# Second MLP product: blocks go on in the same PSUM banks and straight into four output blocks, gate on the sum, first loads ahead of stores

## The chip, the cores and the metric

The kernel runs on one core of one Trainium2 chip. The metric is the device time of one execution in microseconds (us), the median over several runs. A profile is one further execution with the hardware profiler; its own time stands beside its span below.

## What is computed

The reference is one layer of a diffusion backbone block over 1024 latent tokens of width 1024 (a recurrent branch and a Fourier branch, merged), and then the part that matters here:

```python
def sq_relu_mlp(h, w1, w2):
    return jnp.square(jax.nn.relu(h @ w1)) @ w2
...
x = x + gt2 * sq_relu_mlp(modulate(rms_norm(x, g_mlp[i]), sh2, sc2), w1[i], w2[i])
...
return rms_norm(x, g_final)
```

The first MLP product is 1024 x 1024 by 1024 x 4096, the second 1024 x 4096 by 4096 x 1024. gt2 is one row of 1024 factors, the same for all tokens. All inputs are float32.

## The kernel before

Each float32 product is made of three matmuls in the type float32r: an operand is split into a high part (a ScalarE copy that rounds) and a low part (the VectorE difference, both at line 98 in `split`), and `passes` multiplies high by high, high by low and low by high. One matmul is 128 x 128 by 128 x 512.

The MLP runs as block products with seven instead of eight multiplications for a 2 x 2 block product (Strassen in Winograd's form). The first product (class `Pair`, 16 pairs of output rows, lines 902 to 1005) leaves its 32 results as rows of `act_d` in DRAM. For each pair seven products of 12 matmuls each (line 958) go into three PSUM banks, A, B and C; `out3` and `out4` (lines 999 and 992) add the last bank to a sum on VectorE, and `put_out` squares the positive part (line 1004) and stores it (line 1005). A bank is free for other use once that sum has been read.

The second product (class `Mlp2`, line 1017) takes 28 of the 32 rows of the hidden width in three chunks of 5, 5 and 4 blocks k (each block two hidden tiles of 128), and the last four plainly. For each block `load` brings four tiles x, y, z, w from DRAM, each a half of activations and a half of w2 (256 KB each). For each chunk there are seven units u, one for each of the seven products; `split` makes the operands of a unit, `sums` the sums that a later unit needs, `mm` does 12 matmuls for each block into two PSUM tiles of two banks, and `evac` reads them into a page in SBUF. In the loop of `run` the work of step i is recorded as: evac of unit i - 1, loads of the next chunk, split for unit i + 1, sums for unit i + 2, matmuls of unit i.

Before the change each unit has its own PSUM tiles and its own two pages (`acc`, 14 pages): ScalarE copies in the first chunk, VectorE adds in the others (line 1096). At the end `comb` (line 1107) makes the four output blocks out of the seven, 14 sums of 128 x 1024, and `gate` (line 1113) multiplies them by gt2 on GpSimd, 16 halves. The plain part multiplies its four w2 tiles by gt2 (line 1119), and for each of the eight output tiles 24 more matmuls run (line 1179), their result is added to the residual x2 (lines 1163, 1167), and `finish` normalises and stores a tile (lines 1011 to 1015). The last tile is finished in two halves (lines 1261 to 1269).

The order of instructions on TensorE, VectorE and ScalarE in this stage is the order in which the code records them (`tc.manual_schedule`). The order on SyncE, which issues all loads and stores, is set by the framework's scheduler; each load waits until its page is free and, at most eight being under way, for an earlier one. Lines 1252 and 1253 are the passage from the first product to the second:

```python
            mlp2.begin()
            pr[NP - 1].out4()
            psum_pool("psum2", 4)
            mlp2.run()
```

`begin` loads x and z, splits all five blocks of unit 0, loads y and makes the five sums for unit 1. Pages come from the pools `pg` (24, tag s), `yp` (17, tag y) and `wp` (tags wr, wh, wl).

Of the kernel before, what the change touches and what calls it, by code (L numbers as in the profile page):

```python
# [50 lines left out]
def block_kernel(es: ExitStack, tc: tile.TileContext, a, out):  # L51
# [695 lines left out]
    with tc.tile_pool(name="yp", bufs=17, reuse_waits="tile") as yp:  # L747
# [158 lines left out]
        class Pair:  # L906
            def __init__(self, n):
                self.n, self.w = n, {}
# [74 lines left out]
            def p7(self):  # L983
                self.f2 = page([P, T])
# [32 lines left out]
        class Mlp2:  # L1017
# [3 lines left out]
            RING = ("wr",) * 4 + ("y",) * 3 + ("wh", "wl") * 3 + ("s",) * 4  # L1021

            def __init__(self):
                self.units = [(c, u) for c in range(len(self.CHUNKS)) for u in range(7)]
                self.src = [{n: [None] * g for n in "xyzws"} for _, g in self.CHUNKS]
                self.op, self.ps, self.acc, self.slot = {}, {}, [[] for _ in range(7)], 0
# [8 lines left out]
            def load(self, c, names, new=page, ks=None):  # L1035
                n0, g = self.CHUNKS[c]
                for k in ks or range(g):
                    for n in names:
                        r, ca, cb, d = self.SRC[n]
                        t = self.src[c][n][k] = new([P, 2 * HB])  # L1040
                        f = 2 * (n0 + k)
                        dma(t[:, 0:HB], act_d[f + ca][:, r * HB:(r + 1) * HB])
                        dma(t[:, HB:], a["w2"][(f + cb) * P:(f + cb + 1) * P, d * HB:(d + 1) * HB])

            def split(self, i):
# [3 lines left out]
                p, self.op[i] = self.src[c], []  # L1049
                for k in range(self.CHUNKS[c][1]):  # L1050
# [4 lines left out]
                    else:  # L1055
                        split(p["_syyzwx"[u]][k], hi, lo)
                    self.op[i].append((hi, lo))

            def sums(self, i):
# [3 lines left out]
                p = self.src[c]  # L1063
                for k in range(self.CHUNKS[c][1]):
                    x, y, z, w = (p[n][k] for n in "xyzw")
# [12 lines left out]
            def mm(self, i):  # L1078
                self.ps[i] = [mm_ps() for _ in range(2)]
                op, t = self.op.pop(i), [h for ps in self.ps[i] for h in halves(ps)]  # L1080
                for k, hl in enumerate(op):
                    for j in range(4):
                        m = [q[:, j * P:(j + 1) * P] for q in hl]
                        for n, (l, r) in enumerate(passes(m, [q[:, HB:] for q in hl])):
                            PE.matmul(t[j], l, r, start=k == 0 and n == 0, stop=k == len(op) - 1 and n == 2)  # L1085

            def evac(self, i):
# [3 lines left out]
                for j, ps in enumerate(self.ps.pop(i)):  # L1091
                    if c == 0:
                        self.acc[u].append(ypage([P, 2 * HB]))
                        S.activation(self.acc[u][j], ps, AF.Copy)
                    else:
                        V.tensor_tensor(self.acc[u][j], self.acc[u][j], ps, ALU.add)  # L1096

            def begin(self):
                self.load(0, "xz", ypage, range(2))
                self.load(0, "xz", page, range(2, 5))  # L1100
                self.split(0)
                self.load(0, "y")
                self.sums(1)

            def comb(self, d, s0, s1, op):
                for j in range(2):
                    V.tensor_tensor(self.acc[d][j], self.acc[s0][j], self.acc[s1][j], op)  # L1107

            def gate(self, u, d):
                for j in range(2):  # L1110
                    t = self.acc[u][j].rearrange("p (a b) -> p a b", b=HB)
                    for h in range(2):
                        G.tensor_tensor(t[:, h], t[:, h], gt2[:, d * HB:(d + 1) * HB], ALU.mult)  # L1113
# [246 lines left out]
```

## Time and profile before

| | |
|---|---|
| median of 3 runs | 1471.16 us (1470.81 to 1471.35) |
| profiled execution, its own time | 1469.69 us |
| span of its profile | 1467.9 us |
| TensorE (PE), busy | 1390.6 us, 95% |
| VectorE (DVE), busy | 1058.0 us, 72% |
| ScalarE (ACT), busy | 611.2 us, 42% |
| GpSimd (POOL), busy | 123.6 us, 8% |
| granted TensorE clock, mean | 0.983 of full speed |

PE is TensorE's matmuls, PEld its weight loads, SPq SyncE's queue. The span runs from the first to the last instruction; the time of an execution has 1.79 us more. A matmul row shows about 0.39 us from start to end, but matmuls overlap: one starts every 0.23 us. Rows of VectorE overlap a little as well, so the pitch of several in a row is read from a merged row (x5). An arrow "<-" names what ended a wait.

### The profile page before, as it was taken

The numbers are of one execution on the slowest core, as the hardware profiler recorded it, in microseconds if no ns is written. First come the engines' busy times: TensorE is split into PE (matmuls) and PEld (weight loads), VectorE is DVE, ScalarE is ACT, GpSimd is POOL, SyncE is SP. The second block draws the span as 40 slices with busy tenths as digits, with TensorE's granted clock in tenths as the row PEclk, the third lists the DMA queues.
The fourth block names the chain that finished last, engine by engine and source line by source line (L and its number), as shares of the span: only waits on it lengthen the run. The fifth ranks groups of instructions, "written<-read, shape, count | busy, mean of one in ns | idle before, by whom it ended". The sixth has DMA issues, their size and how long they took to land. (4 is left out here: it accounts for less than half of the span.)

```text
span 1467.9 us, 16270 instructions
## 1 busy us (share of the span) xinstructions
PE 1390.6 (95%) x6352; PEld 1131.4 (77%) x6352; DVE 1058.0 (72%) x1209; ACT 611.2 (42%) x753; POOL 123.6 (8%) x62
## 2 busy tenths in 40 slices
PE   4999999999999999999996899999995999999995
PEld 3888788888888878788774678888884888888884
DVE  7664648888887998645656676666665847959998
ACT  7453246665676557321244312222222355333403
POOL 0000000000000000000001100000000320602573
PEclk9999999999999999999998999999998999999998
DMA  8432711333133324648422333332317352042322
GB/s 328 187 115 90 255 49 51 131 131 130 49 126 132 118 80 158 200 132 305 166 86 86 100 129 115 115 115 102 102 61 252 120 181 69 27 149 87 117 84 115
DMA packets 62540, 188.90 MB, mean 129 GB/s; under 512 B 6979, under 2 KB 7387, under 8 KB 62463
## 3 DMA queue, kind: packets, MB, share of 16 engines
q1 hardware_dynamic: 62463, 187.86, 37.1%
q8 instruction: 50, 0.82, 0.2%
q14 instruction: 27, 0.22, 0.0%
HBM read 150.60 MB, written 37.23 MB: 128 GB/s over the span
## 5 line engine op out<-in xcount | busy, mean ns | idle before, releaser
L321 PE MATMUL mm<-pg,wh 128*128 128x512 f32 x1120 | 308.3, 396 | 0.5 <-DVE pg L98 0.5
L321 PEld LDWEIGHTS mm<-pg,wh 128*128 128x128 f32 x1120 | 204.6, 189 | 43.7 <-DVE pg L98 1.0
L958 PE MATMUL bk<-pg,wh 128*128 128x512 f32 x720 | 225.9, 395 | 1.9 <-DVE wr L297 1.1
L321 PE MATMUL mm<-pg,wl 128*128 128x512 f32 x560 | 175.4, 394 | 0.0
L958 PEld LDWEIGHTS bk<-pg,wh 128*128 128x128 f32 x720 | 135.0, 188 | 34.5 <-DVE wr L297 2.1
L958 PE MATMUL bk<-pg,wl 128*128 128x512 f32 x360 | 141.6, 393 | 0.0
L98 DVE TENSOR_TENSOR wl<-wr,wh 128x1024 fp32r<-128x1024 f32 (+2 forms) x73 | 81.6, 1121 | 75.5 <-ACT wh L98 75.5
L98 ACT ACTIVATE wh<-wr 128x1024 fp32r<-128x1024 f32 (+2 forms) x73 | 71.0, 976 | 147.6 <-PE mm L321 67.0
L321 PEld LDWEIGHTS mm<-pg,wl 128*128 128x128 f32 x560 | 105.3, 188 | 24.3
L98 ACT ACTIVATE pg<-pg 128x1024 fp32r<-128x1024 f32 (+4 forms) x86 | 75.7, 901 | 64.5 <-PE mm L1085 13.3
L98 ACT ACTIVATE wh<-pg 128x1024 fp32r<-128x1024 f32 x48 | 50.2, 1061 | 125.7 <-PE bk L958 52.6
L98 DVE TENSOR_TENSOR pg<-pg,pg 128x1024 fp32r<-128x1024 f32 (+4 forms) x71 | 81.0, 1157 | 20.0 <-ACT pg L98 19.9
L859 PE MATMUL mm<-pg,pg 128*128 128x512 f32 x384 | 91.9, 397 | 0.0
L958 PE MATMUL bk<-pg,pg 128*128 128x512 f32 x264 | 72.5, 425 | 19.2 <-ACT pg L98 15.1
L859 PEld LDWEIGHTS mm<-pg,pg 128*128 128x128 f32 x384 | 71.0, 188 | 17.9 <-DVE g L893 2.2
L958 PEld LDWEIGHTS bk<-pg,pg 128*128 128x128 f32 x264 | 52.8, 205 | 35.9 <-ACT pg L98 19.0
L958 PEld LDWEIGHTS bk<-pg,wl 128*128 128x128 f32 x360 | 67.6, 188 | 16.0
L98 DVE TENSOR_TENSOR wl<-pg,wh 128x1024 fp32r<-128x1024 f32 x48 | 58.0, 1223 | 28.0 <-ACT wh L98 28.0
L1074 POOL TENSOR_TENSOR pg<-pg,pg 128x512 f32<-128x512 f32 x14 | 37.5, 2676 | 476.8 <-DVE pg L1072 476.8
L842 POOL TENSOR_TENSOR wr<-pg 128x512 f32<-128x512 f32 x4 | 5.7, 1424 | 810.5 <-ACT pg L823 800.5
L776 PE MATMUL mm<-pg,wh 128*128 128x512 f32 x256 | 70.0, 394 | 1.7 <-ACT pg L98 1.7
L1085 PE MATMUL mm<-pg,pg 128*128 128x512 f32 x224 | 69.7, 392 | 0.0
(279 smaller groups left out, 2659.1 us busy)
## 6 DMA issues: line engine op xcount, KB each, us to landing
wr<-in_win SPq DMA_DIRECT2D x36, 512.0 KB, 4.5
wr<-in_w SPq DMA_DIRECT2D x35, 512.0 KB, 3.6
pg<-in_wm SPq DMA_DIRECT2D x32, 512.0 KB, 8.1
wr<-in_wm SPq DMA_DIRECT2D x32, 512.0 KB, 3.7
act_d<-pg SPq DMA_DIRECT2D x32, 512.0 KB, 2.9
pg<-act_d SPq DMA_DIRECT2D x56, 256.0 KB, 4.8
pg<-in_w SPq DMA_DIRECT2D x56, 256.0 KB, 5.2
pg<-in_x SPq DMA_DIRECT2D x16, 512.0 KB, 8.2
```

The source lines that it names most:

```text
L98: return S.activation(hi, src, AF.Copy), V.tensor_tensor(lo, src, f32(hi), ALU.subtract)
L321: PE.matmul(ps[:, h * HB:(h + 1) * HB], l[:, k, :], r[:, h * HB:(h + 1) * HB], start=k == 0 and i == 0, stop=k == KT - 1 and i == 2)
L776: PE.matmul(ps[:, h * HB:(h + 1) * HB], l[:, k, :], r[:, h * HB:(h + 1) * HB], start=k == 0 and i == 0, stop=k == KT - 1 and i == 2)
L842: G.tensor_tensor(t34[:, 0], b22, b12, ALU.subtract)
L859: PE.matmul(ps, l, r, start=k == 0 and j == 0, stop=k == KT - 1 and j == 2)
L958: PE.matmul(ps, l, r, start=first and k == 0 and i == 0, stop=k == 3 and i == 2, skip_group_check=not first)
L1074: G.tensor_tensor(z[:, HB:], w[:, HB:], y[:, HB:], ALU.subtract)
L1085: PE.matmul(t[j], l, r, start=k == 0 and n == 0, stop=k == len(op) - 1 and n == 2)
```

## The change

- A unit of the second product that goes on from an earlier sum now accumulates on the PSUM tiles of two units before (units 2, 4 and 6 on those of unit 0, unit 3 on those of unit 1; table `ON`). The reordered units are then read straight into four output blocks (table `ACC`; units 2 and 4 subtract, table `SUB`). Eight pages take the place of 14; the combinations at the end are gone.
- `sums` makes other sums, all on VectorE: y + z, y - x, then halves w - y, z - y, y - z and w - y. The last one needs y's right half alone, and the left half of y is loaded once more for the seventh unit.
- gt2 multiplies the sum of an output tile (one product of 128 x 1024 on VectorE) and no longer the blocks and the plain w2 tiles; GpSimd has no work left in this stage.
- The loads of x, z and y of the first chunk are recorded inside the last pair, with higher priority; the splits of unit 0 are recorded as two blocks, then `out4`, then three blocks, then the sums for unit 1.
- The next chunk's tiles are loaded in steps 3 to 6 as x, z, y, w, and w of the first chunk before the loop. Output tiles are finished in the order 0 to 7 instead of 4 to 7, 0 to 3.

```diff
-            RING = ("wr",) * 4 + ("y",) * 3 + ("wh", "wl") * 3 + ("s",) * 4
+            RING = ("wr",) * 4 + ("y",) * 6 + ("wh", "wl") * 3 + ("s",)
+
+            PAGE = "_yyxzwy"
+            ACC = ((0, 0), (1, 1), (0, 1), (0, 1), (1, 1), (0, 0), (1, 0))
+            ON, SUB = (2, 3, 4, 6), (2, 4)
...
                     if u == 1:
-                        p["s"][k] = page([P, 2 * HB])
-                        V.tensor_tensor(p["s"][k], x, y, ALU.subtract)
+                        V.tensor_tensor(y, y, z, ALU.add)
                     elif u == 2:
-                        V.tensor_tensor(y, y, z, ALU.add)
+                        V.tensor_tensor(y, y, x, ALU.subtract)
                     elif u == 3:
-                        V.tensor_tensor(y, y, x, ALU.subtract)
+                        V.tensor_tensor(xl, wl, yl, ALU.subtract)
                     elif u == 4:
-                        G.tensor_tensor(z[:, HB:], w[:, HB:], y[:, HB:], ALU.subtract)
+                        V.tensor_tensor(zl, zl, yl, ALU.subtract)
+                        V.tensor_tensor(zr, yr, zr, ALU.subtract)
                     elif u == 5:
-                        G.tensor_tensor(x[:, 0:HB], w[:, 0:HB], y[:, 0:HB], ALU.subtract)
+                        V.tensor_tensor(yr, wr, yr, ALU.subtract)
+                        self.load_act(y, c, k, 1, 1)
...
-                self.ps[i] = [mm_ps() for _ in range(2)]
+                c, u = self.units[i]
+                self.ps[i] = self.ps[i - 2] if u in self.ON else [mm_ps() for _ in range(2)]
...
-                            PE.matmul(t[j], l, r, start=k == 0 and n == 0, stop=k == len(op) - 1 and n == 2)
+                            PE.matmul(t[j], l, r, start=u not in self.ON and k == 0 and n == 0,
+                                      stop=k == len(op) - 1 and n == 2, skip_group_check=u in self.ON)
...
-                for j, ps in enumerate(self.ps.pop(i)):
-                    if c == 0:
-                        self.acc[u].append(ypage([P, 2 * HB]))
-                        S.activation(self.acc[u][j], ps, AF.Copy)
+                d = self.ACC[u]
+                for j, ps in enumerate(self.ps[i]):
+                    if (d, j) not in self.acc:
+                        t = self.acc[d, j] = ypage([P, 2 * HB])
+                        S.activation(t, ps, AF.Copy, scale=-1.0 if u in self.SUB else 1.0)
                     else:
-                        V.tensor_tensor(self.acc[u][j], self.acc[u][j], ps, ALU.add)
+                        t = self.acc[d, j]
+                        V.tensor_tensor(t, t, ps, ALU.subtract if u in self.SUB else ALU.add)
 
             def begin(self):
-                self.load(0, "xz", ypage, range(2))
-                self.load(0, "xz", page, range(2, 5))
-                self.split(0)
-                self.load(0, "y")
-                self.sums(1)
+                with tc.high_priority(offset=PRIO):
+                    self.load(0, "xz", ypage, range(3))
+                    self.load(0, "xz", page, range(3, 5))
+                    self.load(0, "y")
...
-                G.tensor_tensor(rw, rw, gt2, ALU.mult)
...
-                        V.tensor_tensor(x2[i], x2[i], ps, ALU.add)
+                        for h, s in enumerate(hs):
+                            V.tensor_tensor(t[:, s], z[h], ps[:, s], ALU.add)
+                        V.tensor_tensor(t, t, gt2, ALU.mult)
+                        V.tensor_tensor(x2[i], x2[i], t, ALU.add)
                     else:
...
+                        for h, s in enumerate(hs):
+                            V.tensor_tensor(z[h], z[h], gt2[:, s], ALU.mult)
+                            V.tensor_tensor(x2[i][:, s], x2[i][:, s], z[h], ALU.add)
                             self.plain_mm(self.last[1], i, (h,))
...
                 if nx:
                     nx.s12()
+                else:
+                    c.f2 = page([P, T])
+                    mlp2.begin()
                 c.p7()
...
-            mlp2.begin()
+            mlp2.load(0, "w")
+            mlp2.split(0, range(2))
             pr[NP - 1].out4()
+            mlp2.split(0, range(2, 5))
+            mlp2.sums(1)
...
-            V.tensor_tensor(x2[i][:, s], x2[i][:, s], psl[h], ALU.add)
+            V.tensor_tensor(xg[:, s], psl[h], gt2[:, s], ALU.mult)
+            V.tensor_tensor(x2[i][:, s], x2[i][:, s], xg[:, s], ALU.add)
```

SyncE's queue at the passage from the first product to the second, before (pg_8021 to pg_8048 are x and z of the first chunk, pg_8081 on are y; the stores are values of the last pairs):

```order
L1042 DMA pg_8036<-act_d 128x512
L1043 DMA pg_8036<-in_w 128x512
L1042 DMA pg_8039<-act_d 128x512
L1043 DMA pg_8039<-in_w 128x512
L1005 DMA act_d<-pg_7933 128x1024
L1042 DMA pg_8042<-act_d 128x512
L1043 DMA pg_8042<-in_w 128x512
L1042 DMA pg_8045<-act_d 128x512
L1043 DMA pg_8045<-in_w 128x512
L1042 DMA pg_8048<-act_d 128x512
L1043 DMA pg_8048<-in_w 128x512
L1042 DMA pg_8081<-act_d 128x512
```

The last three rows of y, the first of w and the stores between them, now (pg_8003 to pg_8009 are y, pg_8066 on are w):

```order
L1050 DMA pg_8003<-act_d 128x512
L1047 DMA pg_8003<-in_w 128x512
L1050 DMA pg_8006<-act_d 128x512
L1047 DMA pg_8006<-in_w 128x512
L1050 DMA pg_8009<-act_d 128x512
L1047 DMA pg_8009<-in_w 128x512
L1005 DMA act_d<-pg_7854 128x1024
L1050 DMA pg_8066<-act_d 128x512
L1047 DMA pg_8066<-in_w 128x512
L1050 DMA pg_8069<-act_d 128x512
```

The store of pg_7854 stood between the first two loads and now stands behind all loads of x, z and y; that of pg_7933, which stood inside x and z, now stands inside the loads of w, eight rows further on.

VectorE at the same place, before (pg_7966 is the last value of the last pair, line 993 is `out4`):

```order
L98 TENSOR_TENSOR wr_8058<-pg_8030,wr_8057 128x512
L98 TENSOR_TENSOR pg_8064<-pg_8033,pg_8063 128x512
L98 TENSOR_TENSOR pg_8064<-pg_8036,pg_8063 128x512
L98 TENSOR_TENSOR wh_8070<-pg_8039,pg_8069 128x512
L98 TENSOR_TENSOR wh_8070<-pg_8042,pg_8069 128x512
L98 TENSOR_TENSOR wh_8076<-pg_8045,wl_8075 128x512
L98 TENSOR_TENSOR wh_8076<-pg_8048,wl_8075 128x512
L1068 TENSOR_TENSOR pg_8096<-pg_8021,pg_8081 128x1024
L1068 TENSOR_TENSOR pg_8098<-pg_8027,pg_8084 128x1024
L1068 TENSOR_TENSOR pg_8100<-pg_8033,pg_8087 128x1024
L1068 TENSOR_TENSOR pg_8102<-pg_8039,pg_8090 128x1024
L1068 TENSOR_TENSOR pg_8104<-pg_8045,pg_8093 128x1024
L993 TENSOR_TENSOR pg_7966<-pg_7934,bk_7939 128x512
L1004 SCALAR_TENSOR_TENSOR pg_7966<-pg_7966 128x1024
```

and now:

```order
L98 TENSOR_TENSOR wr_8082<-pg_7967,wr_8081 128x512
L98 TENSOR_TENSOR wr_8082<-pg_7970,wr_8081 128x512
L98 TENSOR_TENSOR wr_8088<-pg_7973,wr_8087 128x512
L98 TENSOR_TENSOR wr_8088<-pg_7976,wr_8087 128x512
L993 TENSOR_TENSOR pg_7966<-pg_7934,bk_7939 128x512
L1004 SCALAR_TENSOR_TENSOR pg_7966<-pg_7966 128x1024
L98 TENSOR_TENSOR pg_8097<-pg_7979,pg_8096 128x512
L98 TENSOR_TENSOR pg_8097<-pg_7982,pg_8096 128x512
L98 TENSOR_TENSOR pg_8103<-pg_7985,pg_8102 128x512
L98 TENSOR_TENSOR pg_8103<-pg_7988,pg_8102 128x512
L98 TENSOR_TENSOR pg_8109<-pg_7991,pg_8108 128x512
L98 TENSOR_TENSOR pg_8109<-pg_7994,pg_8108 128x512
L1074 TENSOR_TENSOR pg_7997<-pg_7997,pg_7970 128x1024
```

Line 993 stood behind ten halves of splits and five whole sums; it now stands behind four halves.

VectorE at the end, before, the last unit's read-out and the first output tile:

```order
L1107 TENSOR_TENSOR pg_8690<-pg_8690,pg_8200 128x1024
L1107 TENSOR_TENSOR pg_8692<-pg_8692,pg_8202 128x1024
L1107 TENSOR_TENSOR pg_8397<-pg_8397,pg_8488 128x1024
L1107 TENSOR_TENSOR pg_8399<-pg_8399,pg_8490 128x1024
L1096 TENSOR_TENSOR pg_8811<-pg_8811,mm_9974 128x1024
L1096 TENSOR_TENSOR pg_8813<-pg_8813,mm_9975 128x1024
L1107 TENSOR_TENSOR pg_8811<-pg_8811,pg_8397 128x1024
L1107 TENSOR_TENSOR pg_8813<-pg_8813,pg_8399 128x1024
L1163 TENSOR_TENSOR x_1503_10032<-x_1503_10032,pg_8589 128x512
L1163 TENSOR_TENSOR x_1503_10032<-x_1503_10032,pg_8306 128x512
L1167 TENSOR_TENSOR x_1503_10032<-x_1503_10032,mm_10075 128x1024
```

and now:

```order
L98 TENSOR_TENSOR pg_9949<-pg_9944,pg_9948 128x1024
L98 TENSOR_TENSOR pg_9951<-pg_9945,pg_9950 128x1024
L1108 TENSOR_TENSOR pg_8812<-pg_8812,mm_9502 128x1024
L1108 TENSOR_TENSOR pg_8814<-pg_8814,mm_9503 128x1024
L1150 TENSOR_TENSOR pg_10024<-pg_8210,mm_10023 128x512
L1150 TENSOR_TENSOR pg_10024<-pg_8395,mm_10023 128x512
L1151 TENSOR_TENSOR pg_10024<-pg_10024,gt_5873 128x1024
L1152 TENSOR_TENSOR x_1455_10004<-x_1455_10004,pg_10024 128x1024
```

No whole sum stands between the last read-out and the first output tile any more, and each tile has one product with gt2 more.

## Rows read from the trace of the kernel before

**Rows 1.** The page: busy time, share of the span and instructions of each engine.

```profile
PE 1390.6 (95%) x6352; PEld 1131.4 (77%) x6352; DVE 1058.0 (72%) x1209; ACT 611.2 (42%) x753; POOL 123.6 (8%) x62
```

**Rows 2.** Chain of waits from 1100 us: start in us, length in us, what.

```profile
1122.20 6.27 DMA pg<-in_w
...
1134.03 1.23 DVE pg L1068
...
1136.54 0.61 DVE pg L993
...
1137.19 227.04 PE mm L1085 x978
...
1364.25 1.22 DVE pg L1096
...
1402.21 5.69 DVE pg L1107 x5
...
1407.96 16.49 POOL pg L1113 x5
```

**Rows 3.** Waits of TensorE from 1137 us: us in total, times, longest.

```profile
PE mm L1085 <- DVE pg L993: 15.5, 1, 15.5
```

**Rows 4.** Windows around the stand: length, busy time by engine, granted clock, DMA share, GB/s.

```profile
1122.00:1137.20 15.20, 0.01 (x1) 0.01 (x1) 10.08 (x13) 6.12 (x7) 0.00 (x0) 0.60 0.74 267
1137.20:1140.00 2.80, 2.80 (x7) 2.22 (x8) 2.80 (x3) 0.00 (x0) 0.00 (x0) 0.50 0.29 114
1140.00:1142.50 2.50, 2.50 (x8) 1.95 (x7) 2.50 (x3) 1.06 (x1) 0.00 (x0) 0.59 0.94 211
```

**Rows 5.** Timeline at the start of the second product: start, length, engine, line, what.

```profile
1065.45 34.45 SPq L1005 DMA_DIRECT2D act_d<-pg  x4
...
1103.51 1.11 SPq L1043 DMA_DIRECT2D pg<-in_w  x1
...
1111.65 0.33 SPq L1043 DMA_DIRECT2D pg<-in_w  x1
...
1118.95 2.49 DVE L98 TENSOR_TENSOR wr<-pg,wr 128x512 fp32r<-128x512 f32 x4
1119.06 0.32 SPq L1005 DMA_DIRECT2D act_d<-pg  x1
...
1119.57 0.40 PE L1085 MATMUL mm<-wr 128*128 128x512 f32 x1
...
1136.45 0.68 DVE L993 TENSOR_TENSOR pg<-pg,bk 128x512 f32<-128x512 f32 x1
```

**Rows 6.** Timeline of VectorE alone and beside GpSimd.

```profile
1145.10 5.76 DVE L1070 TENSOR_TENSOR pg<-pg,pg 128x1024 f32<-128x1024 f32 x5
...
1356.27 4.57 DVE L98 TENSOR_TENSOR pg<-pg,pg 128x1024 fp32r<-128x1024 f32 x2
...
1357.48 2.28 POOL L1076 TENSOR_TENSOR pg<-pg,pg 128x512 f32<-128x512 f32 x1
```

**Rows 7.** Timeline of the end.

```profile
1435.72 17.10 PE L1179 MATMUL mm<-pg,pg 128*128 128x512 f32 x73
...
1450.19 1.28 DVE L1163 TENSOR_TENSOR x<-x,pg 128x512 f32<-128x512 f32 x2
...
1452.91 1.28 DVE L1014 SCALAR_TENSOR_TENSOR x<-x,tiny,gacc 128x1024 f32<-128x1024 f32 x1
...
1461.69 0.68 DVE L1261 TENSOR_TENSOR x<-x,mm 128x512 f32<-128x512 f32 x1
```

**Rows 8.** Window over the whole second product, columns as in rows 4.

```profile
1120.00:1468.00 348.00, 317.06 (x1367) 258.20 (x1367) 283.59 (x249) 131.51 (x154) 110.61 (x48) 0.96 0.33 114
```

**Rows 9.** The page: DMA issues, count, KB each, median us from issue to landing.

```profile
act_d<-pg SPq DMA_DIRECT2D x32, 512.0 KB, 2.9
pg<-act_d SPq DMA_DIRECT2D x56, 256.0 KB, 4.8
pg<-in_w SPq DMA_DIRECT2D x56, 256.0 KB, 5.2
```

More of the change, by code (lines that the diff above doesn't have):

```diff
@@ L983, in p7 @@
             def p7(self):
-                self.f2 = page([P, T])
+                self.f2 = page([P, T]) if self.f2 is None else self.f2
                 self.mm(self.B, "s3", "t3", False)
@@ L1048, in split @@
                 c, u = self.units[i]
-                p, self.op[i] = self.src[c], []
-                for k in range(self.CHUNKS[c][1]):
+                p, op = self.src[c], self.op.setdefault(i, [])
+                for k in ks or range(self.CHUNKS[c][1]):
                     hi, lo = self.ring(), self.ring()
@@ L1055, in split @@
                     else:
-                        split(p["_syyzwx"[u]][k], hi, lo)
-                    self.op[i].append((hi, lo))
+                        split(p[self.PAGE[u]][k], hi, lo)
+                    op.append((hi, lo))
             def sums(self, i):
@@ L1125, in run @@
             def run(self):
-                nu, nc_, self.pl = len(self.units), len(self.CHUNKS), []
+                nu, last = len(self.units), len(self.CHUNKS) - 1
                 f0 = 2 * sum(self.CHUNKS[-1])
@@ L1129, in run @@
                     self.evac(i - 1)
-                    if u == 1:
-                        self.load(c, "w")
-                    if u >= 4 and c + 1 < nc_:
-                        self.load(c + 1, "xyz"[u - 4])
+                    if u >= 3 and c < last:
+                        self.load(c + 1, "xzyw"[u - 3])
                     self.split(i + 1)
                     self.sums(i + 2)
-                    if c + 1 == nc_ and u >= 3:
+                    if u >= 3 and c == last:
                         self.plain(f0 + u - 3)
@@ L1138, in run @@
                     self.mm(i)
-                order = (4, 5, 6, 7, 0, 1, 2, 3)
-                Q1, Q7, Q5, Q6, Q4, Q2, Q3 = range(7)
                 for j in range(KT):
-                    x2[j] = wp.tile([P, D], F32, tag=self.RING[(0, 1, 2, 3, 7, 8, 9, 10)[j]], name=nm("x2"),
-                                    bufs=4 if j < 4 else 3)
+                    tag = ("wr",) * 4 + ("wh", "wl") * 2
+                    x2[j] = wp.tile([P, D], F32, tag=tag[j], name=nm("x2"), bufs=4 if j < 4 else 3)
@@ L1155, in run @@
-                self.evac(nu - 1)
-                self.comb(Q3, Q3, Q5, ALU.add)
-                self.gate(Q3, 1)
-                C = ((Q2, Q3), (Q4, Q7))
-                for n, i in enumerate(order):
-                    for h in range(2):
-                        s = slice(h * HB, (h + 1) * HB)
-                        t = self.acc[C[i // 4][h]][i % 4 // 2][:, i % 2 * HB:(i % 2 + 1) * HB]
-                        V.tensor_tensor(x2[i][:, s], x2[i][:, s], t, ALU.add)
-                    if n < KT - 1:
-                        ps = mm_ps()
+                self.evac(nu - 1)
@@ L1168, in run @@
                     else:
                         self.last = i, [mm_ps()[:, 0:HB] for _ in range(2)]
-                        for h in range(2):
+                        for h, s in enumerate(hs):
+                            V.tensor_tensor(z[h], z[h], gt2[:, s], ALU.mult)
+                            V.tensor_tensor(x2[i][:, s], x2[i][:, s], z[h], ALU.add)
                             self.plain_mm(self.last[1], i, (h,))
-                    if n:
-                        finish(order[n - 1])
+                    if i:
+                        finish(i - 1)
```

44 lines of the change are left out of this document (17 added, 27 removed).

## The prediction

> **What bounds the kernel now.** I read the page first: TensorE is busy 95% of the span [rows 1], so time can come only from the places where it stands or runs slowly, and from what follows its last matmul. The chain of waits from 1100 us to the end, in order of time, names two [rows 2]. Between 1122 and 1137 us the chain leaves TensorE: it goes through landing loads, the sums of line 1068 and line 993 on VectorE, and comes back to TensorE for a long unbroken piece. From 1364 us on it never returns to TensorE: it runs through VectorE, its combinations at line 1107, GpSimd's gates at line 1113 and VectorE again until the end. The list of waits confirms the first: one wait of 15.5 us, on line 993 [rows 3]. There is no other wait of TensorE behind 1137 us.
>
> The timeline tells why [rows 5]. The last first-product pair puts its last value out at line 993, which frees the bank that the second tile of unit 0 needs. VectorE takes it only after all ten halves of unit 0's splits and the five sums for unit 1. Those wait for loads, and the loads stand on SyncE behind the store of line 1005 at 1119.06 us, itself waiting for VectorE; the load before it left at 1111.65 us. TensorE does six matmuls, then stands.
>
> The stand costs more than itself. The granted clock is 0.50 (the 1.2 GHz level) from 1137.2 to 1140 us, and the next 2.5 us show a mean of 0.59 [rows 4]: 2.8 + 2.5 × 0.41 / 0.5 = 4.85 us at half speed, half of it lost, **2.4 us**.
>
> The end: the last matmul ends at 1435.72 + 17.10 = 1452.8 us [rows 7], 15.1 us before the span does.
>
> TensorE's pace without disturbance: the second product is 14 × 7 × 12 + 8 × 24 = 1368 matmuls (the window over the stage has 1367 of them [rows 8]); all but six ran from 1137.2 to 1452.8 us. (315.6 − 2.4) / 1362 = **0.230 us** each.
>
> **The change part by part.** *The start.* The loads of x, z and y now stand ahead of the last three stores of line 1005. Four have left earlier still, and 26 follow the store that ended a long wait of SyncE at 1065.45 + 34.45 = 1099.9 us and lands 2.9 us later, at 1103 [rows 5, 9], because the first of them takes over its page. Before, 12 loads left from 1103.5 to 1111.65 us, 0.7 us apart, and took about 5 us to land [rows 5, 9]. So x and z are there by 1103 + 16 × 0.7 + 5.2 = 1119.5 us, the first y at 1121 and the last at 1126 us. Pages of z's last block and of y come free only inside the last pair, whose seven products of 12 matmuls end at 1119.6 us: the third of them, which reads t1 last, ends 4 × 2.76 us earlier, at 1108.5, ahead of their turn. VectorE runs four halves of splits to 1118.95 + 2.49 = 1121.4 us as before [rows 5]; behind these comes line 993, 0.68 us, instead of behind eleven more. TensorE's second tile can start at 1122.15 us; before, that same matmul started at 1137.2 [rows 2]. Six matmuls from 1119.57 us [rows 5] end at 1121.6, so a stand of 0.6 us is left: gain 1137.2 − 1122.15 = **15.0 us**, and **2.4 us** because the clock should not fall.
>
> What is late next: unit 0 lasts until 1122.15 + 54 × 0.230 = 1134.6 us. VectorE then has line 1004 (1.2), six halves (3.7, at 0.62 each), five sums y + z (5.75, at 5.76 / 5 = 1.15 each [rows 6]) and the first split of unit 1: ready at 1134.0 us. That is 0.6 us of slack, the tightest place. Each later block asks 1.15 us of VectorE against 2.76 of TensorE, so the slack grows.
>
> *The units.* Matmuls are the same in number and size. The four continuing units of a chunk write on a bank that was read out one unit earlier, 13.8 us; only the order decides, so I cost it at nothing. Fourteen fresh read-outs by ScalarE become eight, so VectorE has 34 instead of 28. Per chunk of five VectorE now has 30 whole and 10 half splits, 10 whole and 20 half sums, and 14 read-outs: 54 × 1.15 + 30 × 0.62 = 80.7 us against 420 × 0.230 = 96.6 us of TensorE. The heaviest unit has 2 read-outs, 5 splits and 10 half sums, 14.2 us against 13.8; the lightest have 8. Splits run a unit ahead, so 0.4 us is swallowed. Cost nothing; without that cover, a few times 0.4 us.
>
> GpSimd falls idle in this stage, and that is worth something: beside its halves of 2.28 us each, VectorE's splits took 4.57 / 2 = 2.3 us instead of 1.15 [rows 6]. So moving 28 half sums to VectorE (28 × 0.62 = 17 us) gives back about 28 × 1.15 = 32 us there. The Trainium skill says otherwise in Perfetto Trace Analysis, section Optimizing Scalar/DVE Operations: "if DVE is saturated, offloading some work to Scalar (or even GPSIMD) may make sense", though it adds that between these two it might not help. By that rule the sum would lose what rival A loses; by the row it loses nothing.
>
> The five reloads of y's left half per chunk, 256 KB each, wait on SyncE for the difference at the new line 1080; the loads of the next z, y and w stand behind them. I reckon that difference at 1166 us and the ten z halves landed by 1180, wanted at 1206: nothing. The stage needs VectorE only 284 of 348 us before [rows 8], and less now.
>
> *The end.* The combinations (14 whole sums, 16 us) and 16 gates (16.5 us of the chain for five of them alone [rows 2]) go. Each output tile now costs VectorE two halves out of the bank (1.3), the gate product and the sum (2.4 with the hand-overs), and reciprocal and scaling (1.4): 5.1 us against 24 × 0.230 = 5.5 us of TensorE. Before, the same loop without the gate took 1452.91 − 1450.19 + 1.2 = 3.9 us [rows 7], but started late. So TensorE sets the pace to its end, E = 1122.15 + 1362 × 0.230 = 1435.4 us. Then VectorE's queue: the scaling of tile 5 and a gated half run to E + 0.9; then five halves, a reciprocal, a half, the scaling of tile 6 (1.3) and the last sum: 7 × 0.61 + 0.1 + 1.3 = 5.6, so E + 6.5. From the end of that sum (line 1261, 1461.69 + 0.68) the span had 5.5 us left before [rows 7]: square, root, scale, store. End E + 12.0 = 1447.4 us, so **3.1 us** are gained behind the last matmul. Bounds: 9 us, if the scaling of tile 6 gets out of the way, to 15.1 as now.
>
> **Sum:** 15.0 + 2.4 + 3.1 = 20.5 us off a span of 1467.9. The profiled execution itself took 1469.69 us, so 1449.2; the median of the runs is 1471.16, 1.5 above it, and on its scale I forecast **1450.7, say 1451 us**. The end alone moves this from 1448 to 1454.
>
> **The rivals.** *A, VectorE becomes the bound.* For it: heavy units ask 14.2 us of 13.8, and each split also waits for ScalarE. If that wait is 0.3 us per block, nine heavy units run 1.7 us over and TensorE waits 15 us in all: 1466 us. Against it: the sum per chunk has 16 us of slack, and VectorE loses GpSimd's interference. It is the case that the Trainium skill's rule in Perfetto Trace Analysis, section Optimizing Scalar/DVE Operations, warns of. It decides only if the lead of one unit is used up at the start. Chance 0.08.
>
> *B, the loads come no earlier.* The order puts them ahead, but their pages must be free; if SyncE is held by one page until the last pair's end, the loads come as before, while line 993 is early all the same. The sums for unit 1 would then end at 1136.4 us [rows 5], its first split at 1137.6, 3 us behind TensorE; with as much again over the next blocks and the clock's 2.4 that is 8.4 us: 1459 us. For it: six tiles wait for products of the last pair. Against: the product they wait for ends at 1108.5 us. Chance 0.07.
>
> *C, slower: the reloads hold SyncE's queue at both chunk borders.* If z of the next chunk lands 16 us too late twice, each border costs what the start costs now, 15.5 + 2.4: 1450.7 + 36 = 1486 us. It needs the difference of line 1080 to run 40 us later than I reckon, since z has 26 us in hand; slower than before needs both borders, over 20 us in sum. Nothing in the rows points there. Chance 0.03.
>
> **How the numbers follow.** Forecast 0.82, A 0.08, B 0.07, C 0.03. The range 1446 to 1460 holds the forecast with its end terms and B, and leaves out most of A and C. About 0.2% (3 us) is what a measurement of this kernel can tell from no change: faster by more 0.93 (forecast, B, nearly all of A), within it 0.03 (A at its worst), slower 0.04 (C, and A at twice its price).
>
> **What would show it.** Right: no wait of TensorE over 1 us between 1119 us and its last matmul; clock 1.00 throughout that stretch; the first unit 0 matmul on its second tile near 1122 us; matmuls ending near 1435 us; 12 us behind them; VectorE's whole sums at 1.15 us everywhere. Wrong: a wait on line 98 at the head of units (A), a stand near 1122 to 1130 us with a half clock behind it (B), waits on loads near 1206 and 1300 us (C), or more than 15 us behind the last matmul.

## The result and the profile after

| | before | after |
|---|---|---|
| median | 1470.99 us of 4 runs (1469.38 to 1471.35) | 1449.51 us of 4 runs (1448.78 to 1450.85) |
| ratio, 95% interval | | 0.9857 (0.9840 to 0.9874) |
| profiled execution, span | 1469.69 us, 1467.9 us | 1448.78 us, 1447.0 us |

The forecast was 1451 us, 1446 to 1460; the profiled execution was forecast at 1449.2 and took 1448.78.

The page of the changed kernel, busy time by engine (answers to [rows 1]): GpSimd has lost 110.6 us of work, TensorE stands less.

```profile
PE 1385.9 (96%) x6352; PEld 1128.9 (78%) x6352; DVE 1045.1 (72%) x1254; ACT 605.3 (42%) x747; POOL 13.0 (1%) x14
```

All waits of TensorE from 1119 us to the end (answers to [rows 3]): 0.7 us in all where one wait took 15.5.

```profile
PE mm L1094 <- DVE pg L993: 0.4, 1, 0.4
PE mm L1094 <- DVE wr L98: 0.3, 1, 0.3
```

The chain of waits (answers to [rows 2]): behind line 993 it runs on TensorE for 307 us, through the units and the plain part, and leaves it only for the last tiles. No piece goes over GpSimd.

```profile
1119.63 2.49 DVE wr L98 x4
1122.12 0.61 DVE pg L993
...
1122.77 267.66 PE mm L1094 x1170
1390.44 39.13 PE mm L1166 x168
...
1429.59 1.29 DVE pg L1150 x2
```

Windows over the same stretch (answers to [rows 4, 8]; the third figure from the end is the granted clock): 1.00 throughout, the 2.4 GHz level.

```profile
1119.60:1122.80 3.20, 2.50 (x11) 1.43 (x9) 3.17 (x7) 1.12 (x3) 0.00 (x0) 1.00 1.03 380
1122.80:1140.00 17.20, 17.20 (x76) 14.19 (x77) 17.20 (x18) 7.25 (x7) 0.00 (x0) 1.00 1.01 374
...
1160.00:1435.00 275.00, 275.00 (x1201) 224.99 (x1199) 223.73 (x238) 102.19 (x120) 0.00 (x0) 1.00 0.33 113
```

The timelines of SyncE and VectorE at the start (answer to [rows 5]). The last load of y leaves at 1120.31 us, the store of pair 14 only behind it, at 1120.98. VectorE goes from line 993 through splits, sums (1.15 us each) and the first splits of unit 1 without a gap.

```profile
1120.31 0.33 SPq L1047 DMA_DIRECT2D pg<-in_w  x1
1120.98 0.33 SPq L1005 DMA_DIRECT2D act_d<-pg  x1
```

```profile
1122.04 0.68 DVE L993 TENSOR_TENSOR pg<-pg,bk 128x512 f32<-128x512 f32 x1
...
1123.90 3.69 DVE L98 TENSOR_TENSOR pg<-pg,pg 128x512 fp32r<-128x512 f32 x6
1127.51 5.75 DVE L1074 TENSOR_TENSOR pg<-pg,pg 128x1024 f32<-128x1024 f32 x5
1133.19 3.48 DVE L98 TENSOR_TENSOR wl<-pg,wh 128x1024 fp32r<-128x1024 f32 x3
```

The timeline of the end (answers to [rows 7]). The last matmul ends at 1404.70 + 30.40 = 1435.10 us, and VectorE is busy from there until the last sum at 1440.63.

```profile
1404.70 30.40 PE L1166 MATMUL mm<-pg,pg 128*128 128x512 f32 x130
...
1433.97 1.27 DVE L1014 SCALAR_TENSOR_TENSOR x<-x,tiny,gacc 128x1024 f32<-128x1024 f32 x1
...
1435.16 0.68 DVE L1156 TENSOR_TENSOR pg<-pg,gt 128x512 f32<-128x512 f32 x1
...
1439.43 1.27 DVE L1014 SCALAR_TENSOR_TENSOR x<-x,tiny,gacc 128x1024 f32<-128x1024 f32 x1
1440.63 0.68 DVE L1255 TENSOR_TENSOR x<-x,pg 128x512 f32<-128x512 f32 x1
```

### The profile page after: what moved, and what is told of

The parts are those of the page before. It is cut to its first block, busy times and chain, and to the rows that moved or that the text cites. A ratio compares the mean times of both kernels' runs of the same rounds, so it can differ in the third digit from the quotient of the medians.

```text
span 1447.0 us, 16245 instructions
## 1 busy us (share of the span) xinstructions
PE 1385.9 (96%) x6352; PEld 1128.9 (78%) x6352; DVE 1045.1 (72%) x1254; ACT 605.3 (42%) x747; POOL 13.0 (1%) x14
## 5 line engine op out<-in xcount | busy, mean ns | idle before, releaser
L98 DVE TENSOR_TENSOR wl<-wr,wh 128x1024 fp32r<-128x1024 f32 (+2 forms) x73 | 81.5, 1119 | 76.6 <-ACT wh L98 76.5
L98 ACT ACTIVATE wh<-pg 128x1024 fp32r<-128x1024 f32 (+1 forms) x52 | 52.4, 1027 | 141.0 <-PE bk L958 52.7
L859 PE MATMUL mm<-pg,pg 128*128 128x512 f32 x384 | 91.9, 397 | 0.0
L958 PE MATMUL bk<-pg,pg 128*128 128x512 f32 x264 | 71.1, 419 | 19.7 <-ACT pg L98 15.1
L98 DVE TENSOR_TENSOR pg<-pg,pg 128x1024 fp32r<-128x1024 f32 (+4 forms) x79 | 73.8, 969 | 18.0 <-ACT pg L98 17.9
L98 DVE TENSOR_TENSOR wl<-pg,wh 128x1024 fp32r<-128x1024 f32 (+1 forms) x52 | 60.2, 1178 | 22.9 <-ACT wh L98 22.9
L1094 PE MATMUL mm<-pg,pg 128*128 128x512 f32 x240 | 74.1, 390 | 0.0
L1108 DVE TENSOR_TENSOR pg<-pg,mm 128x1024 f32<-128x1024 f32 x34 | 41.0, 1218 | 39.4 <-PE mm L1094 38.3
L1094 PE MATMUL mm<-pg 128*128 128x512 f32 x164 | 64.1, 391 | 0.0
```

Source lines behind the costliest of these rows:

```text
L98: return S.activation(hi, src, AF.Copy), V.tensor_tensor(lo, src, f32(hi), ALU.subtract)
L859: PE.matmul(ps, l, r, start=k == 0 and j == 0, stop=k == KT - 1 and j == 2)
L958: PE.matmul(ps, l, r, start=first and k == 0 and i == 0, stop=k == 3 and i == 2, skip_group_check=not first)
L1094: PE.matmul(t[j], l, r, start=u not in self.ON and k == 0 and n == 0, stop=k == len(op) - 1 and n == 2, skip_group_check=u in self.ON)
L1108: V.tensor_tensor(t, t, ps, ALU.subtract if u in self.SUB else ALU.add)
```

## The experiments

Where the first matmul of the second product starts differs by some us between profiled executions (1119.57 before, 1122.57 in out4_only, whose code ahead of it is the same; 1123.74 in start_three), so I read each trace from there: **matmuls** is the time from that start to the end of the last matmul, **behind** the time from there to the end of the span, both read from TensorE's timeline. A stand in the last pair lies ahead of that start and is in neither. "Stand" is TensorE's longest wait from 1095 us on. Ratios are to runs of the kernel before on the same chip (medians 1471.0 for the changed kernel, 1471.3 for the four rows below it, 1472.2 for the others). Medians of different groups can thus differ by 1.3 us without any change, so I give gains against each group's own runs of the kernel before.

| kernel | stand, at | matmuls | behind | median | ratio (95%) |
|---|---|---|---|---|---|
| before | 15.5, unit 0 | 333.3 | 15.1 | 1471.0 | 1 |
| changed | 0.4, unit 0 | 314.8 | 11.9 | 1449.5 | 0.9857 (0.9840 to 0.9874) |
| out4_only | 3.9, unit 1 | 321.6 | 15.0 | 1460.0 | 0.9925 (0.9908 to 0.9941) |
| loads_only | 13.4, last pair; 9.7, unit 0 | 327.5 | 15.2 | 1480.5 | 1.0068 (1.0053 to 1.0083) |
| start_only | 13.1, last pair | 315.8 | 15.1 | 1469.7 | 0.9987 (0.9978 to 0.9997) |
| late_start | 12.0, unit 0 | 328.7 | 11.9 | 1463.1 | 0.9948 (0.9932 to 0.9965) |
| two_blocks | 13.0, last pair | 314.9 | 11.9 | 1466.3 | 0.9958 (0.9941 to 0.9975) |
| start_three | 0.4, unit 0 | 315.9 | 14.9 | 1454.2 | 0.9880 (0.9865 to 0.9894) |
| out4_back | 9.7, unit 0 | 326.0 | 11.9 | 1461.2 | 0.9922 (0.9908 to 0.9937) |
| gate_on_gpsimd | 3.6, first tile | 320.7 | 7.3 | 1451.0 | 0.9859 (0.9845 to 0.9872) |
| gate_on_sum_only | 14.5, unit 0 | 332.7 | 15.8 | 1472.2 | 1.0004 (0.9995 to 1.0012) |
| sums_on_gpsimd | 0.4, unit 0 | 314.9 | 11.8 | 1450.0 | 0.9855 (0.9840 to 0.9870) |
| short_tail | 0.4, unit 0 | 314.8 | 9.1 | 1446.6 | 0.9831 (0.9817 to 0.9845) |
| gpsimd_tail | 2.4, first tile | 319.9 | 6.9 | 1449.2 | 0.9848 (0.9833 to 0.9863) |

**The start in parts, on the kernel before.** out4_only records line 993 behind two blocks of splits:

```diff
-                self.split(0)
+                self.split(0, range(2))
+                pr[NP - 1].out4()
+                self.split(0, range(2, 5))
                 self.load(0, "y")
...
             mlp2.begin()
-            pr[NP - 1].out4()
```

> The kernel before with one thing altered: line 993 (out4) of the last pair is recorded behind the first two blocks of unit 0's splits; the loads stay where they were. Theory O (VectorE's order is the main part, the loads only guard what follows): the second tile of unit 0 starts near 1122 us as in the changed kernel; y still lands late, so the five sums end near 1136.4 us as before and the first split of unit 1 near 1137.6, against a unit 0 that ends at 1134.6: one new stand of about 3 us at the head of unit 1, on line 98. With the clock kept the gain is 15 + 2.4 - 3 = 14 us, with the clock lost 12: 1457 to 1459 us. Theory L (the loads are the main part): TensorE stands on the missing halves inside unit 0 and on the sums, over 10 us in all, and the time is 1465 us or more. The end stays as before, 15 us behind the last matmul.

loads_only and start_only load inside the last pair, as the change does; start_only has the order of out4_only too:

```diff
             def begin(self):
-                self.load(0, "xz", ypage, range(2))
-                self.load(0, "xz", page, range(2, 5))
-                self.split(0)
-                self.load(0, "y")
-                self.sums(1)
+                with tc.high_priority(offset=PRIO):
+                    self.load(0, "xz", ypage, range(2))
+                    self.load(0, "xz", page, range(2, 5))
+                    self.load(0, "y")
...
                 if nx:
                     nx.s12()
+                else:
+                    c.f2 = page([P, T])
+                    mlp2.begin()
                 c.p7()
...
```

> The kernel before with one thing altered: x, z and y of the first chunk are loaded inside the last pair, ahead of its stores; line 993 stays behind ten halves of splits and five sums. Theory O: VectorE runs ten halves and five sums without a gap from 1119 to about 1131.5 us, then line 993; TensorE stands from 1121.6 to about 1132.2, 10.5 us, and the clock still falls to 0.50 behind it: gain about 5 us, 1466 us. Theory L: the loads were what line 993 waited for, so the stand goes by most of its 15.5 us: 1456 us or less.

> The kernel before with both parts of the start and nothing else of the change (own tiles for each unit, 14 sums at the end, gate of the blocks on GpSimd). If start and end add up as in the prediction: the stand goes (14.4 to 15 us) and the slow clock behind it (2.4), and everything behind is shifted by that, with 15 us behind the last matmul as before: 1471 - 17.4 = 1453.5 us. If the new second product is worth something in its middle as well (a steadier TensorE), this run stays above that by as much; if its added VectorE work costs something, the run comes below 1453.

out4_only did as theory O said, with a stand of 3.9 us for 3 and the clock lost behind it (0.60 in the 4 us behind): 11.7 us gained from the first matmul to the end. The early loads did not: loads_only is slower than the kernel before, and start_only gains 0.1%. At unit 0 both have about what I had worked out (start_only 0.4 us, loads_only 9.7 for 10.5), and a stand of 13 us ahead of it, in the last pair, that no theory had. The timelines of SyncE and VectorE in start_only show its cause:

```profile
1121.79 0.33 SPq L1043 DMA_DIRECT2D pg<-in_w  x1
1122.52 15.03 SPq L1005 DMA_DIRECT2D act_d<-pg  x2
```

```profile
1108.96 0.69 DVE L977 TENSOR_TENSOR pg<-pg,bk 128x512 f32<-128x512 f32 x1 [3.22 <-PE bk L958]
1128.48 0.69 DVE L986 TENSOR_TENSOR pg<-pg,bk 128x512 f32<-128x512 f32 x1 [18.83 <-DMA act_d<-pg]
```

Line 986 (`p7` of the last pair) writes its sum on a page that a store of `put_out` still reads. That store had its value at 1105.8 us, but stands on SyncE behind all loads of x, z and y, leaves at 1122.5 and lands 5.84 us later, at 1128.4. Bank C is not read out until then, and TensorE stands. Windows of start_only, over the stand and behind it: the granted clock falls to 0.50, the 1.2 GHz level.

```profile
1117.00:1129.90 12.90, 0.00 (x0) 0.00 (x0) 1.38 (x2) 0.00 (x0) 0.00 (x0) 0.66 0.81 303
1129.90:1132.70 2.80, 2.75 (x7) 2.17 (x8) 0.00 (x0) 1.07 (x3) 0.00 (x0) 0.50 0.00 0
```

**Whose page.** The changed kernel moves the same store behind the same loads and has no such stand. It puts x and z of three blocks, not two, into pages of yp, where eight output pages take the place of 14; so its early loads take nine pages of pg, those of start_only eleven. Two runs change that number alone. two_blocks, on the changed kernel:

```diff
-                    self.load(0, "xz", ypage, range(3))
-                    self.load(0, "xz", page, range(3, 5))
+                    self.load(0, "xz", ypage, range(2))
+                    self.load(0, "xz", page, range(2, 5))
```

> The changed kernel with x and z of two blocks, not three, in pages of the pool yp (as before the change); two more pages of pg are taken by the early loads, and the sum of line 986 in the last pair then has to write on the page that the store of pair 14's last value still reads, a store that now stands behind all early loads. Theory P (pages): in start_only that wait, not the sums at the end or the banks, ate the gain; here the stand of 13 us in the last pair comes back, with the half clock behind it: 1449.5 + 13.1 + 2.5 = 1465 us. Theory M (the new second product is what makes the early start pay, by fewer units' pages and steadier matmuls): no such stand, 1449 to 1451 us.

start_three is the reverse edit on start_only.

> start_only with x and z of three blocks in pages of yp: the kernel before, both parts of the start, nothing of the new second product. Theory P: line 986 waits for no store any more, no stand in the last pair, 0.4 us at the second tile of unit 0, and everything behind is shifted: 15 us behind the last matmul as before, 1453 to 1454 us. Theory M: 1465 us or more, by a stand in the last pair or by one in the first chunk, where 14 pages of read-out and the third block's x and z meet in yp.

Both came out by theory P, to 1.3 us. TensorE's waits in two_blocks, and then in start_three:

```profile
PE bk L958 <- DVE pg L987: 13.0, 1, 13.0
PE mm L1094 <- DVE pg L993: 0.4, 1, 0.4
```

```profile
PE mm L1086 <- DVE pg L993: 0.4, 1, 0.4
```

So two pages decide over 15 to 17 us of the changed kernel (16.7 between the medians 1466.3 and 1449.5, 14.9 by the ratios 0.9958 and 0.9857), and with them the start needs nothing else of the change: start_three gains 18.0 us on the kernel before, of the changed kernel's 21.5.

**The start taken out of the changed kernel.** late_start loads and splits x, z, y behind the last pair, with line 993 behind ten halves and five sums; out4_back moves line 993 alone back there:

```diff
             mlp2.load(0, "w")
-            mlp2.split(0, range(2))
+            mlp2.split(0)
+            mlp2.sums(1)
             pr[NP - 1].out4()
-            mlp2.split(0, range(2, 5))
-            mlp2.sums(1)
```

> The changed kernel with its start put back: x, z, y are loaded and split behind the last pair, line 993 behind ten halves and five sums. If the parts add up: the stand of 15.5 us and the slow clock of 4.85 us come back and 12 us stay behind the last matmul: 1449.5 + 17.5 = 1467 us, 4 us under the kernel before. If the end gains nothing by itself (because VectorE is late there only when it is behind already), it is 1470 to 1471.

> The changed kernel with line 993 put back behind ten halves and five sums, the early loads kept. VectorE runs them without a gap from 1119.6 to 1131.5 us, then line 993 until 1132.2: one stand of 9.9 us at the second tile of unit 0 and a half clock behind it (2.4 us): 1449.5 + 9.5 + 2.4 = 1461.5 us. If the loads were what counted: under 1453.

out4_back hit (1461.2). late_start came out 4 us faster than expected: its stand is 12.0 us, not 15.5. On its SyncE timeline 18 loads of x and z, not 14, leave ahead of the store that holds SyncE up (at 1120.17 us, before at 1119.06); I put this down to the third block in yp. Four loads fewer behind that store, 0.7 us apart, account for 2.8 of the 3.5 us. Its 11.9 us behind the last matmul show that the end's gain doesn't hang on the start. With the early loads but without the early line 993, 11.0 of the changed kernel's 21.5 us are left (1472.2 to 1461.2); with the early line 993 but without the early loads (out4_only), 4 us of stand remain.

**GpSimd and the middle.** sums_on_gpsimd puts the twenty half sums of a chunk, four lines, on GpSimd; the first:

```diff
-                        V.tensor_tensor(xl, wl, yl, ALU.subtract)
+                        G.tensor_tensor(xl, wl, yl, ALU.subtract)
...
```

> The changed kernel with all twenty half sums of a chunk (new lines 1078, 1080, 1081, 1083) on GpSimd. Theory 1: GpSimd needs 46 us of the 97 of a chunk and VectorE's operations beside it take 2.3 instead of 1.15 us; VectorE is then at 68 + 23 = 91 us of 97, the reloads of y wait some 14 us longer and z of the next chunk lands near 1195 of 1206 us: TensorE sees nothing of it, 1449 to 1451 us. Rival A of the prediction in another form: VectorE is held up in the heavy units, waits on line 98 appear at the head of units, 1455 to 1466 us.

The time stayed (1450.0) and no wait of TensorE over 0.4 us came. VectorE now waited up to 3.54 us at a time for ScalarE's high parts, and ScalarE up to 3.7 us for GpSimd's sums, but TensorE, which takes the splits a unit later, felt none of it. Nor did VectorE win anything. Window from 1120 us to the end, of the changed kernel and of sums_on_gpsimd: without 56 half sums (56 × 0.60 = 34 us) VectorE (the third busy time of a row) has 1.7 us less.

```profile
1120.00:1447.00 327.00, 314.41 (x1370) 256.65 (x1368) 271.50 (x295) 124.87 (x147) 0.00 (x0) 0.99 0.36 126
```

```profile
1120.00:1447.00 327.00, 314.47 (x1370) 256.86 (x1369) 269.77 (x239) 124.93 (x147) 120.89 (x56) 0.99 0.35 126
```

**The end.** gate_on_gpsimd puts the gates of blocks and plain tiles back on GpSimd, gate_on_sum_only takes them from there in the kernel before. The core of the first, in `evac` of the last chunk and in `run`:

```diff
+                        for h in range(2):
+                            G.tensor_tensor(th[:, h], th[:, h], gt2[:, d[1] * HB:(d[1] + 1) * HB], ALU.mult)
...
-                            V.tensor_tensor(t[:, s], z[h], ps[:, s], ALU.add)
-                        V.tensor_tensor(t, t, gt2, ALU.mult)
-                        V.tensor_tensor(x2[i], x2[i], t, ALU.add)
+                            V.tensor_tensor(x2[i][:, s], x2[i][:, s], z[h], ALU.add)
+                        V.tensor_tensor(x2[i], x2[i], ps, ALU.add)
```

> The changed kernel, but gt2 is multiplied as before on GpSimd: 16 halves on the four output blocks as each is read out for the last time, and the four plain w2 tiles; an output tile then takes two halves and one whole sum on VectorE, 3.9 instead of 5.1 us. Theory 1 (the tail is VectorE's chain behind the last matmul, and the gate on the sum lengthens it): the gates of the early blocks hide in units 4 to 6, the last four are done by 1400 us against tile 4 at 1415; VectorE is ahead of TensorE at the end and 7 to 8 us stay behind the last matmul: 1445.5 us. Theory 2 (the gates on GpSimd were what made the old end late, beside the combinations): GpSimd slows VectorE's splits and read-outs to 2.3 us in the last units, the first tiles start late, and the time is 1450 or more.

> The kernel before with the gate alone moved: gt2 times the sum on VectorE, no gates on GpSimd; own tiles and the 14 sums stay, the start too. Theory 1: VectorE's splits of 2.3 to 3.4 us beside GpSimd shrink to 1.2, so it comes to the 14 sums some us earlier, but then needs 5.1 us for each of eight tiles from about 1418 us on: it still sets the end, which comes 2 to 5 us earlier than before, 1466 to 1469 us. Theory 2 (GpSimd's gates alone made the old end late): VectorE keeps up with TensorE and the end is 12 us behind the last matmul as in the changed kernel, gain over 3 us and no chain through VectorE from 1364 us on.

gate_on_gpsimd has the short end of theory 1 (7.3 us) but missed its 1445.5 us: its matmuls take 5.9 us longer than the changed kernel's. Waits of TensorE and GpSimd's timeline: the last plain w2 tile is multiplied behind four gates of a block, and the first output tile waits for its split.

```profile
PE mm L1169 <- ACT pg L98: 3.6, 1, 3.6
```

```profile
1389.48 6.02 POOL L1112 TENSOR_TENSOR pg<-pg,gt 128x512 f32<-128x512 f32 x4 [3.57 <-DVE pg L1108]
1395.46 2.33 POOL L1124 TENSOR_TENSOR pg<-pg,gt 128x1024 f32<-128x1024 f32 x1
```

gate_on_sum_only gained nothing, so its expected 1466 to 1469 us was missed. VectorE does the 14 sums as before and then needs 5.1 us a tile; besides, its step for the first half of the last tile stood ahead of tile 6's and waited 3.19 us for TensorE, so what taking the gates off GpSimd is worth by itself stays open. The pair points at the 14 sums as what held the old end up: with the sums and without gates on GpSimd the end stays long (15.8 us), with those gates and without the sums it is short (7.3). The two kernels also differ in the order of the output tiles and in the product with gt2 for each tile, and no run takes out the sums alone, so this is argued from two runs and not shown by one.

gpsimd_tail tried to mend gate_on_gpsimd: plain tiles first, and the last tile's residual takes its blocks behind tile 4.

```diff
                         self.plain(f0 + u - 3)
+                    if i:
+                        self.gate(i - 1)
                     self.mm(i)
```

> gate_on_gpsimd with two edits: each plain w2 tile is multiplied before the block gates of its step (so that the split of the last one no longer waits for them), and the residual of the last output tile takes its block sums behind tile 4, not behind the last matmul. Expected: no wait of TensorE at the first output tile (3.6 us and 1.5 us of slow clock there go), and 7 us behind the last matmul in place of 11.9 of the changed kernel, 9.1 of short_tail: 1449.5 - 5 = 1444.5 us. If GpSimd's gates still come late, or slow VectorE's last read-outs, 1447 or more.

The end shrank to 6.9 us as expected, the stand did not go, and 1444.5 us was missed: three of the four gates still ran ahead of the last plain tile (GpSimd's order is the framework's, not the code's), which came at 1393.48 instead of 1395.46. Stands of 2.4 and 0.5 us, and a clock of 0.58 over the 3.7 us behind them, ate the gain.

short_tail keeps the gate on the sum and reorders VectorE's last steps (behind the last matmul: both sums, the scaling of tile 6, the products with g_final):

```diff
                         self.last = i, [mm_ps()[:, 0:HB] for _ in range(2)]
+                        for h in range(2):
+                            self.plain_mm(self.last[1], i, (h,))
+                    if i == 0:
+                        n = KT - 1
                         for h, s in enumerate(hs):
-                            V.tensor_tensor(z[h], z[h], gt2[:, s], ALU.mult)
-                            V.tensor_tensor(x2[i][:, s], x2[i][:, s], z[h], ALU.add)
-                            self.plain_mm(self.last[1], i, (h,))
-                    if i:
+                            z = self.acc[(1, h), 1][:, HB:]
+                            V.tensor_tensor(z, z, gt2[:, s], ALU.mult)
+                            V.tensor_tensor(x2[n][:, s], x2[n][:, s], z, ALU.add)
+                    elif i < KT - 1:
                         finish(i - 1)
...
```

> The changed kernel with its last steps in another order: residual and gated block product of the last output tile are added right behind tile 0, where VectorE stands over 4 us; behind the last matmul come the two gated halves, the two sums, then the scaling of tile 6, then the rest. Theory: 11.9 us behind the last matmul are VectorE's queue (10 halves and one scaling ahead of the last square), of which four halves (2.4 us) go and the scaling gets out of the way of the last sum by some 0.6: 8.5 to 9.3 us, 1446.5 us. Rival: the end is set by squares, root and store behind the last sum of the first half or by the store of tile 6, and nothing over 1 us is gained.

It hit: 9.1 us behind the last matmul, 1446.6 us, a gain of 25.6 us on its own runs of the kernel before. Its four runs (1445.35 to 1448.23) lie below all four of the changed kernel, though the intervals of the two ratios still touch; the 2.8 us behind the last matmul are the surer figure. Its timeline: both last sums have ended 1438.43 + 1.28 = 1439.7 us, 2.4 behind the last matmul (1437.33), where the changed kernel took 1440.63 + 0.68 - 1435.10 = 6.2; the scaling of tile 6 comes behind them.

```profile
1437.24 1.27 DVE L1260 TENSOR_TENSOR pg<-mm,gt 128x512 f32<-128x512 f32 x2
1438.43 1.28 DVE L1262 TENSOR_TENSOR x<-x,pg 128x512 f32<-128x512 f32 x2
...
1439.63 1.28 DVE L1264 SCALAR_TENSOR_TENSOR x<-x,tiny,gacc 128x1024 f32<-128x1024 f32 x1
```

## Why the prediction was right, point by point

- **The stand, 15.0 us.** Line 993 was forecast to let the second tile start at 1122.15 us, 2.6 behind the first matmul; it started at 1122.77, 2.5 behind it. Against 17.6 before that is 15.1. Three things were needed for that: without the early order (out4_back) 9.7 us of stand remain, without the early loads (out4_only) 3.9 at unit 1, without the pages (two_blocks) 13.0 in the last pair. start_three has all three and nothing else, and no stand over 0.4 us.
- **The clock, 2.4 us.** It stayed at 1.00, so this came back. Matmuls took 18.4 us less in all, 0.9 more than 15.1 + 2.4. start_three, with the old units, takes 1.1 us longer than the changed kernel (315.9 against 314.8) at the same stands and the same clock of 1.00, and so it goes for start_only with the old units (315.8), two_blocks and short_tail with the new (314.9, 314.8): the new units are about 1 us quicker, which the sum had at nothing. What in them is quicker stays open.
- **The end, 3.1 us.** 15.1 became 11.9. The order of VectorE's last steps was as the prediction put it, and the pace of tiles TensorE's (5.59 us). Of its bounds, 9 us "if the scaling of tile 6 gets out of the way" is what short_tail reached, by that and four halves less.
- **The units, nothing.** No wait on line 98 over 0.3 us, at the chunk borders none at all. The tightest place, the first split of unit 1, was ready at 1133.19 + 1.15 = 1134.3 us of 1122.77 + 54 × 0.229 = 1135.1, 0.8 us of slack for 0.6.
- **Rival A** fell: in the changed kernel no wait on line 98 at the head of a unit came, and in sums_on_gpsimd, which moves the sums the other way, the time stayed. The rule of the Trainium skill that it leaned on (Perfetto Trace Analysis, section Optimizing Scalar/DVE Operations) held in its second half alone, that between these two engines moving work might not help: 271.50 against 269.77 us on VectorE.
- **Rival B** fell in the form I gave it, loads that come no earlier. The real danger beside it was missing. "The order puts them ahead, but their pages must be free" looked at the pages that loads wait for, not at who waits for the page of a store that the loads overtake. Where the order in front of the prediction showed the store of pg_7854 behind all loads, the sum had no term for its waiter. It is worth 0 here and 15 to 17 us with two pages of yp less. At this place the forecast held by luck: its working doesn't show why no stand came.
- **Rival C** did not come: no wait at a chunk border, and the differences of line 1080 ended at 1164.4 us, forecast 1166.

## What to carry to other kernels

When loads are put ahead of stores, find for each overtaken store the instruction that next writes its page, and who waits for that; here two pages decided whether it was nothing or 13 us. Two causes of one wait (an order and a transfer) are not worth the sum of what each brings alone: apart they gave 11 and -9 us here, together, with the pages for it, 18. What follows the last matmul is one engine's queue: take out of it what could run in that engine's earlier gaps.

## What the runs showed of the hardware

VectorE and GpSimd held each other up here when both read two operands from SBUF, and not evenly. In sums_on_gpsimd a half sum that takes GpSimd 1.3 us alone took 11.06 while VectorE ran sums and splits back to back, unslowed; later three splits took 6.80 us in place of 3.48, about 1.1 us more for each, and five halves 11.26. First GpSimd's timeline, then VectorE's:

```profile
1140.42 11.06 POOL L1078 TENSOR_TENSOR pg<-pg,pg 128x512 f32<-128x512 f32 x1 [312.33 <-DVE pg L1076]
1151.43 1.30 POOL L1080 TENSOR_TENSOR pg<-pg,pg 128x512 f32<-128x512 f32 x1
...
1174.01 11.26 POOL L1083 TENSOR_TENSOR pg<-pg,pg 128x512 f32<-128x512 f32 x5
```

```profile
1138.90 5.75 DVE L1076 TENSOR_TENSOR pg<-pg,pg 128x1024 f32<-128x1024 f32 x5
...
1177.31 6.80 DVE L98 TENSOR_TENSOR wl<-pg,wh 128x1024 fp32r<-128x1024 f32 x3
```

The prediction had taken 2.3 us for every VectorE operation beside GpSimd [rows 6]; that is one of two regimes, and which one comes was not settled. Sums that read a bank were not slowed: in gate_on_gpsimd the sum of a bank into the residual took 1.22 us beside GpSimd's gates (1401.36 to 1407.29 us), and 1.22 later without them:

```profile
1404.99 1.22 DVE L1156 TENSOR_TENSOR x<-x,mm 128x1024 f32<-128x1024 f32 x1
1408.54 1.22 DVE L1156 TENSOR_TENSOR x<-x,mm 128x1024 f32<-128x1024 f32 x1
```

The Trainium skill has both in SBUF — State Buffer, section Who interferes with whom: a VectorE instruction with two inputs in SBUF and a GpSimd instruction that reads SBUF lock each other out for a whole instruction, one with a single SBUF input does not contend. These rows agree; why a GpSimd half lost its turn to some nine VectorE operations running, and later took every second one, stays open.

Stands of 2.4 and 0.5 us (gpsimd_tail), 3.6 us (gate_on_gpsimd) and 3.9 us (out4_only) were each followed by a clock of 0.58 to 0.73 in the next 4 to 5 us, as these windows show; the stands of 0.4 and 0.3 us at unit 0 were not (1.00 in the changed kernel).

```profile
1398.30:1402.00 3.70, 3.70 (x10) 2.94 (x11) 3.70 (x4) 0.00 (x0) 2.60 (x2) 0.58 0.02 4
1399.90:1405.00 5.10, 4.84 (x17) 3.88 (x17) 5.00 (x6) 0.00 (x0) 3.64 (x3) 0.73 0.02 3
1142.00:1146.00 4.00, 4.00 (x11) 3.19 (x12) 4.00 (x4) 1.69 (x2) 0.00 (x0) 0.60 0.74 264
```
